# A hybrid pooling and linear-attention trunk: hand-ordered stages with barriers, against a list-scheduled rewrite with wider blocks and folded weights

## The chip, the cores and the metric

One Trainium2 chip, all 8 cores of it, one batch element on each core. The time is that of the slowest core, in device microseconds (us). A program on all cores has two states. In the slow one, the cores of a die show a lower granted TensorE clock and the run is longer: of the changed kernel's four runs one took 2278.8 us, with a mean clock of 0.92 to 0.94 on one die, against 2212.47 to 2216.9.

## The reference, cut to what matters

Four layers on 2048 tokens plus 16 meta tokens, width 1024, inner width 2048. Layers 0 and 2 are pooling mixers, layers 1 and 3 gated linear attention (GLA).

```python
def pool_mixer(h, w_in, w_grp, scale, w_out):
    u, z = split(h @ w_in)                                   # 2048 each
    t = trailing_mean(u, windows 2, 4, 8, 16 by group) - u   # linear in u, along the tokens
    y = einsum('blgc,gcd->blgd', t, w_grp)                   # 512 x 512 in each of 4 groups
    return (y * scale * silu(z)) @ w_out

def gla_mixer(h, w_in, w_gate2, b_gate, head_norm, w_out):   # 4 heads, chunk by chunk
    cum = cumsum(log_sigmoid(glr @ w_gate2 + b_gate) / 16)   # within a chunk
    qe, ke = q * exp(cum), k * exp(-cum)
    o = tril(qe @ ke.T) @ v + qe @ S
    S = exp(g_tot) * S + (k * exp(g_tot - cum)).T @ v
    return (rmsnorm_head(o) * head_norm * silu(z)) @ w_out

h = h + mixer(rmsnorm(h, norm), ...)                         # per layer; a last rmsnorm at the end
```

Two facts carry the change. The window mean runs along tokens and `w_grp` along channels, so `w_grp` may be applied before the window, that is, multiplied into `w_in` once. And the next layer's `rmsnorm` of a token tile needs only that tile's finished `h`.

## The kernel before

Every engine has its own instruction list. The order in each list is the order in which the program states its operations. A record of readers and writers of each buffer puts in the semaphore waits. Ahead of each layer stands a norm pass over all 17 token tiles, between barriers:

```python
def prepass(gvec_ap, gla):
    ...
    P.barrier()
    hnbs = [hnb, arena[:, 0:512].bitcast(BF16)]     # two buffers for the normalised tile, in turn
    ...
    for i in range(NT):
        pT = body(i)          # DVE: h * rstd * gain -> hnbs[i % 2]; PE: 8 transposes into bank i % 2
        if i + 2 < NT:
            stats(i + 2)      # ACT: square with sum, ln, exp
        evac(i, pT)           # ACT: PSUM -> hnT

def pool_layer(li, ui0):
    prepass(pool_norm[j:j + 1, :], False)
    ...
    P.barrier()
    def stageB(bi):           # the group matmul, 16 instructions per 256 tokens
        for oc in range(4):
            for fc in range(4):
                ins = e.matmul(py[:, oc, 0:n], lhsT=Wg[:, fc, ...], rhs=T[par][:, fc, 0:n], ...)
```

## Time and profile before

| | before |
|---|---|
| median of 3 runs | 2314.25 us (2313.78 to 2317.47) |
| TensorE busy, profiled run | 2144.0 us, 93% of 2317.0 |
| until the first projection | 89.6 us |
| three norm passes between layers | some 94 us |
| pool block, 256 tokens | 12.19 us |
| GLA, 128 tokens | 9.00 us |

The lines behind the table stand in the prediction. The columns are the engine and line that waited, what it waited for, then the total us, the number of times and the longest.

```profile
PE ps L377 <- DVE hnb L368: 86.4, 19, 18.5
PE ps L532 <- ACT arena L476: 15.2, 6, 2.8
```

The first line is the norm pass (line 377 is its transposes), 86.4 us in 19 waits, most of it at the start. Nothing else comes near. Within the layers TensorE hardly waits: the time is the work itself, and the way to a shorter time is less of it, and no passes in between.

### The profile page before, as it was taken

To read this page: it belongs to the slowest core of one execution; us is meant where nothing else is said; L and a number is where in the kernel's file an instruction comes from. 1 tells how busy PE (TensorE), PEld (TensorE's weight loads), DVE (VectorE), ACT (ScalarE), POOL (GpSimd) and SP (SyncE) were. 2 spreads that over 40 slices of the span, in tenths; PEclk is the share of its full clock that TensorE was granted. 3 is DMA by queue.
4 is the path that set the end of the run, shared out by engine and by line. 5 is a ranking of instruction groups with operands and counts; after the bars stand their busy time and mean duration, and the time that the engine had idled before them with its cause. 6 is when DMAs were issued, how large, how long until landed. Compare 5 with 4: busy or idle time off the path is not lost.

```text
span 2317.0 us, 60097 instructions; the slowest of 8 cores (2307.8 to 2317.0 us)
## 1 busy us (share of the span) xinstructions
PE 2144.0 (93%) x22136; PEld 1563.1 (67%) x22136; DVE 1420.2 (61%) x2844; ACT 1168.2 (50%) x2579; POOL 360.4 (16%) x254
## 2 busy tenths in 40 slices
PE   1599999997999999999979999999799999999997
PEld 1477767675776776766657777777567677677675
DVE  3354544455777776767773544444657777677787
ACT  3321111235766676667763111113557676676787
POOL 0012234560000000000001133456200000000000
PEclk9999999998999999999979999999899999999998
DMA  9303040404004004030030030313400210400011
GB/s 220 68 12 63 3 65 1 74 11 73 2 2 75 2 4 72 2 59 9 2 65 12 1 65 1 65 21 54 74 11 2 42 34 2 75 2 2 29 57 65
DMA packets 14801, 86.67 MB, mean 37 GB/s; under 512 B 2498, under 2 KB 2498, under 8 KB 6324
## 3 DMA queue, kind: packets, MB, share of 16 engines
q0 software_dynamic: 9664, 63.31, 16.8%
q1 hardware_dynamic: 4852, 19.51, 2.5%
q8 instruction: 184, 3.01, 0.5%
q14 instruction: 101, 0.83, 0.1%
HBM read 137.47 MB, written 8.39 MB: 63 GB/s over the span
## 4 chain that ended last, share of the span: by engine, by line
PE 85%; DVE 4%; ACT 4%; issue 4%; DMA 2%; another core or an unknown queue 1%; DVEq 0%; POOL 0%; ACTq 0%; SPq 0%; POOLq 0%
PE ps L467 20%; PE ps L713 10%; PE ps L555 10%; PE ps L728 10%; PE ps L846 9%; PE ps L742 9%; PE ps L532 6%; PE ps L806 2%; PE ps L787 2%; DMA W<-wpack 2%; PE ps L783 1%; PE ps L680 1%; PE ps L377 1%; PE ps L829 1%
## 5 line engine op out<-in xcount | busy, mean ns | idle before, releaser
L467 PE MATMUL ps<-hnT,W 128*128 128x256 bf16 (+1 forms) x4608 | 476.1, 263 | 11.8 <-DVE arena L537 9.0
L467 PEld LDWEIGHTS ps<-hnT,W 128*128 128x128 bf16 x4608 | 416.2, 98 | 77.2 <-issue 17.1
L484 POOL TENSOR_TENSOR arena<-arena 128x1048 f32<-128x1048 f32 (+9 forms) x180 | 323.2, 1796 | 610.9 <-ACT arena L478 552.3
L537 DVE SCALAR_TENSOR_TENSOR arena<-ps,pscale,arena 128x256 bf16<-128x256 f32 (+1 forms) x288 | 131.4, 456 | 407.6 <-PE ps L532 384.0
L478 ACT ACTIVATE arena<-ps 128x1024 f32<-128x1024 f32 (+1 forms) x72 | 67.4, 936 | 417.3 <-PE ps L467 417.2
L846 PE MATMUL ps<-W,arena 128*128 128x512 bf16 (+1 forms) x1088 | 263.1, 386 | 0.0
L713 PE MATMUL ps<-hnT,W 128*128 128x128 bf16 (+1 forms) x4352 | 260.6, 217 | 0.0
L728 PE MATMUL ps<-W,hnT 128*128 128x512 bf16 (+1 forms) x1088 | 260.5, 383 | 0.0
L742 PE MATMUL ps<-hnT,W 128*128 128x128 bf16 (+1 forms) x4352 | 256.9, 216 | 0.0
L555 PE MATMUL ps<-W,arena 128*128 128x512 bf16 (+1 forms) x1088 | 255.3, 389 | 0.0
L713 PEld LDWEIGHTS ps<-hnT,W 128*128 128x128 bf16 x4352 | 244.5, 99 | 0.2
L742 PEld LDWEIGHTS ps<-hnT,W 128*128 128x128 bf16 x4352 | 236.7, 97 | 0.5
L850 DVE SCALAR_TENSOR_TENSOR h<-ps,arena,h 128x512 f32<-128x512 f32 (+1 forms) x272 | 203.7, 749 | 33.9 <-PE ps L846 8.0
L731 ACT ACTIVATE arena<-ps 128x512 bf16<-128x512 f32 (+1 forms) x136 | 81.1, 597 | 282.1 <-PE ps L728 279.3
L796 DVE SCALAR_TENSOR_TENSOR arena<-ps,hnorm,arena 128x128 bf16<-128x128 f32 (+1 forms) x544 | 187.0, 344 | 58.9 <-DVE arena L796 1.6
L298 POOL DMA_DIRECT2D W<-wpack x64 | 34.3, 547 | 1025.0 <-PE ps L829 932.0
L728 PEld LDWEIGHTS ps<-W,hnT 128*128 128x128 bf16 (+1 forms) x1088 | 105.2, 98 | 130.6 <-issue 6.9
L559 DVE TENSOR_TENSOR h<-h,ps 128x512 f32<-128x512 f32 (+1 forms) x272 | 180.5, 683 | 16.6 <-PE ps L555 3.4
L555 PEld LDWEIGHTS ps<-W,arena 128*128 128x128 bf16 (+1 forms) x1088 | 107.4, 100 | 122.7 <-issue 17.5
L812 DVE SCALAR_TENSOR_TENSOR arena<-arena,ps 128x512 f32<-128x512 f32 x240 | 178.3, 743 | 12.9 <-DVE arena L812 0.5
L846 PEld LDWEIGHTS ps<-W,arena 128*128 128x128 bf16 (+1 forms) x1088 | 100.6, 98 | 101.6 <-issue 6.0
L532 PE MATMUL ps<-arena,W 128*128 128x256 bf16 (+1 forms) x1152 | 140.0, 277 | 23.1 <-ACT arena L476 15.2
(96 smaller groups left out, 2778.6 us busy)
## 6 DMA issues: line engine op xcount, KB each, us to landing
W<-wpack POOLq DMA_DIRECT2D x56, 1024.0 KB, 16.9
h<-x SPq DMA_DIRECT2D x8, 1024.0 KB, 33.4
out<-h SPq DMA_DIRECT2D x16, 512.0 KB, 2.6
W<-wpack POOLq DMA_DIRECT2D x8, 512.0 KB, 19.8
gbc<-pool_norm SPq DMA_DIRECT2D x2, 512.0 KB
gbc<-gla_norm SPq DMA_DIRECT2D x2, 512.0 KB
gbc<-final_norm SPq DMA_DIRECT2D x1, 512.0 KB
arena<-cst POOLq DMA_DIRECT2D x1, 128.0 KB, 6.5
```

The source lines that it names most:

```text
L467: ins = e.matmul(dst[:, fc, 0:n], lhsT=Wuz[:, kc, off + fc * 128:off + (fc + 1) * 128], rhs=hnT[:, kc, c0:c0 + n], start=(kc == 0), stop=( ...
L484: add = lambda dst, a, b: (lambda e: e.tensor_tensor(out=dst, in0=a, in1=b, op=ALU.add))
L532: ins = e.matmul(py[:, oc, 0:n], lhsT=Wg[:, fc, oc * 128:(oc + 1) * 128], rhs=T[par][:, fc, 0:n], start=(fc == 0), stop=(fc == 3))
L555: ins = e.matmul(po[0:nt, :], lhsT=Y[par][:, oc, cc:cc + nt], rhs=Wo[:, oc, half * 512:(half + 1) * 512], start=(oc == 0), stop=(oc == 3))
L559: P.op("dve", lambda e, half=half, nt=nt, ti=ti, po=po: e.tensor_tensor(out=h[0:nt, ti, half * 512:(half + 1) * 512], in0=h[0:nt, ti, half ...
L713: ins = e.matmul(pq[:, idx * 2 + dc, 0:n], lhsT=Wm[:, kc, dc * 128:(dc + 1) * 128], rhs=hnT[:, kc, c0:c0 + n], start=(kc == 0), stop=(kc = ...
L728: ins = e.matmul(pv[0:n, :], lhsT=hnT[:, kc, c0:c0 + n], rhs=Wv[:, kc, :], start=(kc == 0), stop=(kc == 7))
L742: ins = e.matmul(pz[:, ec, 0:n], lhsT=Wz[:, kc, ec * 128:(ec + 1) * 128], rhs=hnT[:, kc, c0:c0 + n], start=(kc == 0), stop=(kc == 7))
L796: P.op("dve", lambda e, ec=ec: e.scalar_tensor_tensor(out=yT[par][:, ec, 0:n], in0=po[:, ec, 0:n], scalar=hnorm[:, hd * 4 + ec:hd * 4 + ec ...
L812: P.op("dve", lambda e, dc=dc: e.scalar_tensor_tensor(out=S[:, dc, :], in0=S[:, dc, :], scalar=Eq[par][:, dc, n - 1:n], in1=pS[dc][:, :], ...
L846: ins = e.matmul(pout[0:n, :], lhsT=yT[par][:, ec, 0:n], rhs=Wo[:, ec, half * 512:(half + 1) * 512], start=(ec == 0), stop=(ec == 3))
L850: P.op("dve", lambda e, half=half, pout=pout: e.scalar_tensor_tensor(out=h[0:n, ti, half * 512:(half + 1) * 512], in0=pout[0:n, :], scalar ...
```

## The change

The intent is to drop work that TensorE needn't do and to let the norm of the next layer run inside the last group or head of this one. A rewrite; its core:

```diff
-    def barrier(self, engs=("pe", "act", "dve")):
+    def schedule(self):        # list scheduling of all operations with modelled durations
+        ...                    # an engine takes the ready operation that the program states first
-        P.op("pe", mmg, [bT[par], Wb[s][1]], PB(0, 1))           # group matmul per block
+    def fold(ui):              # w_in[:, group] @ w_grp, once for each group: 32 matmuls of 512
-        blocks = [(0, NMETA, [0])] + [(NMETA + NB * b, NB, ...)]  # meta, 8 x 256; GLA: 17 tiles
+BLOCKS = [([0, 1], 0, 144)] + [... 7 x 256 ...] + [([16], 1936, 128)]
-                        e.matmul(pcum[:, dc, 0:n], lhsT=lhi[...], rhs=tri[0:n, 0:n], ...)
+                    e.tensor_tensor_scan(out=Eq[...], data0=ones[...], data1=la[...], ...)  # DVE
-        S = exp(g) * S + kd.T @ v          # k scaled by exp(g_tot - cum)
+        S = el_prev * S + ke.T @ v         # k as it is; the decay goes into the copy that is read
+                    act([A["S"], b_el], [A["Sb"]], Sb[...], S[...], AF.Copy, scale=el[:, dc, k:k + 1])
-    hnbs = [hnb, arena[:, 0:512].bitcast(BF16)]
+    hnb = [sb("hnb0", [128, D], BF16)]      # one buffer, also where the square's output goes
-                  [(lambda q, k=k: q.dma_start(out=h[:, 1 + 2 * k:3 + 2 * k, :], ...   # x: 8 x 1 MB
+        dma("sp", "x%d" % i, h[:, i - 1, :], xv[:, i - 1, :], ...)                     # x: 16 x 512 KB
```

In the new GLA layer:

```python
def chunk(k_, k, t_, o, m):                          # one tile of 128 tokens in one head
    mm([b_ke, b_qe], [bank[4]], ...scores...)        # PSUM bank 4
    tr([b_ke, b_const], [bank[4]], ...k...)          # PSUM bank 4
    ...                                              # output: bank 5; state, projection: banks 6, 7
    if hd == 3:
        after_tile(li, t_)

def after_tile(li, t_):
    norm_tile(t_, 4)                                 # the next layer's norm: transposes in bank 4
```

## The prediction

> **What bounds the kernel now.** I read the page first: busy time by engine, the 40 slices, the chain that ended last. Then the trace: windows by stage, the matmul timeline for the cost of one instruction, the timeline of a norm pass for the cost of its hops.
>
> ```profile
> PE 2144.0 (93%) x22136; PEld 1563.1 (67%) x22136; DVE 1420.2 (61%) x2844; ACT 1168.2 (50%) x2579; POOL 360.4 (16%) x254
> PE   1599999997999999999979999999799999999997
> PE 85%; DVE 4%; ACT 4%; issue 4%; DMA 2%; another core or an unknown queue 1%; DVEq 0%; POOL 0%; ACTq 0%; SPq 0%; POOLq 0%
> ```
>
> TensorE is the bound: 85% of the chain is matmuls. The holes are the first slice and three dips between layers. The windows give their size (start, a pool group, norm pass, a GLA head, norm pass; columns: length, then busy time of PE, weight loads, DVE, ACT, POOL, granted clock, DMA share, GB/s):
>
> ```profile
> 0.00:89.60 89.60, 16.54 (x136) 12.70 (x137) 31.06 (x37) 34.15 (x71) 5.68 (x14) 1.00 0.83 186
> 307.70:417.00 109.30, 106.26 (x858) 79.55 (x857) 51.35 (x104) 18.25 (x27) 49.52 (x32) 0.95 0.22 35
> 529.50:562.00 32.50, 20.81 (x274) 16.24 (x273) 21.80 (x18) 23.31 (x45) 0.53 (x1) 0.88 0.50 92
> 870.00:1025.00 155.00, 154.17 (x1845) 109.55 (x1843) 110.31 (x237) 105.89 (x256) 2.11 (x4) 0.99 0.18 30
> 1191.00:1219.60 28.60, 16.56 (x138) 12.72 (x139) 22.39 (x18) 18.85 (x24) 0.53 (x1) 0.50 0.48 78
> ```
>
> 89.6 us pass before the first projection; a norm pass is 28 to 33 us of little matmul work, after which the clock is 0.50; inside the layers TensorE has no air. Its steady price, from the chain in order of time:
>
> ```profile
> 121.91 3.45 PE ps L555 x16
> 125.37 6.99 PE ps L467 x64
> 134.10 3.45 PE ps L555 x16
> ```
>
> L467 streams 256 columns: 6.99/64 = 109.2 ns each. L555 streams 512: 3.45/16 = 215.6. The block period is 134.10 - 121.91 = 12.19 us, of which 12.19 - 6.99 - 3.45 = 1.75 is the group matmul (16 x 109.2). With 128 columns, L713 x32 starts at 1174.99 and its successor at 1176.78: 55.9 ns. With 16 columns 29.7 (563.38 to 564.33, x32), with one 27.5. GLA's period is 9.00 us per 128 tokens (632.31 to 641.31).
>
> Counting the program and multiplying: 5256 x 109.2 + 11536 x 55.9 + 3520 x 215.6 + 1280 x 29.7 + 544 x 27.5 = 2031 us. The span is 2317, so 286 us are not matmul streaming: some 80 at the start, about 58 in three norm passes (94 us less some 36 of transposes and gate-input matmuls), the rest (near 148) group and head boundaries, half-clock stretches behind them, and the tail.
>
> **What the Trainium skill says.** "TensorE: Matmul & The Clock Gate", section "Wait — 56ns, not 53.3ns?": back-to-back spacing is N/2.4 ns + about 2.5 ns. The trace agrees: 109.2, 215.6, 55.9. Same page, "Part 1: The HAM clock gate": after an idle window of about 3.4 us the array runs at half clock until it has been busy for as long. The trace agrees: clock 0.50 at 1191 to 1219.6, and behind a 2.5 us gap at 190.37 sixteen matmuls of 256 columns took 3.57 us. The same section warns of a peak-current limiter at 13/16 of the clock once three cores of a die run dense matmuls. The trace shows it only in short bursts: 0.81 at 450 to 455 us on this core, none on die 0. "ScalarE: Activation LUTs", "What ACT_TABLE_LOAD costs": a per-partition pointer operand adds about 93 ns; L733's 398 ns at 128 columns against 365 for 256 columns without one (L682) fits.
>
> **The change, part by part.**
>
> Group matmul folded. It drops 1152 matmuls (1024 x 109.2 + 128 x 29.7 = 116 us) and adds 8 folds of 32 x 215.6 = 6.9 us, 55 us. Net -61.
>
> 256-token blocks. GLA's q, k, z go from 128 columns to 256: 8192 x 55.9 = 458 becomes 3584 x 109.2 + 512 x 62.5 (144 columns, an estimate by the formula) + 512 x 55.9 = 452: only -6. The pool layers' first and last block are 144 and 128 instead of 256: +5. The meta tile's own 16-column projections go (1024 x 29.7 = -30), and its output projection turns from 128 matmuls of 512 columns into 224 of 16: -21.
>
> Gates transposed with scan: the 512 + 32 cumulative-sum matmuls go (-30), ScalarE and VectorE take over. Gate input on wider blocks: a few us at most. The parts add up to -143 or so.
>
> All counted from the built program: 7392 of 256, 3648 of 512, 3616 of 128, 1056 of 144, 488 of 16, 512 of 1: 1890 us. Streaming falls by 140.
>
> Other engines, at the durations of before. ScalarE in GLA per 256 tokens: gate 0.91 + 0.63 + 1.26, v 1.19, z by exp-ln-exp 3.70, kd 0.73, square 1.16, the scaled state copy 4 x 0.72, head norm 0.89: 13.4 us. VectorE: q, k 1.39, z 4 x 0.484, mask 0.57, y 1.38, state 2.97, output 3.0, scan 4 x 0.34 (estimate): 12.6. TensorE: 64 x 109.2 + 36 x 215.6 + 32 x 55.9 + 2 x 109.2 + 8 x 27.5 = 17.0. So both lie beside it. In the fourth head each tile adds a norm: ScalarE +5.5 per block, 18.9 against TensorE's 17.9: there ScalarE binds by 1 us a block, some 8 us in one layer. Pool block: TensorE 12.19 - 1.75 = 10.44; ScalarE 5.6; VectorE 6.6; GpSimd with window 16 four adds of 2.03 plus a copy, 8.4, close but under.
>
> No barriers, norms in the stream: the three passes (58 us) and most boundaries go. Their transposes remain in the 1890.
>
> The start. This I expect NOT to improve. In the built order TensorE's first fold stands behind the transposes of all 16 tiles, and the changed kernel has one normalised-tile buffer, which is also the junk output of the square. So a tile's chain must close before the next begins. Its hops, here before the second pool layer:
>
> ```profile
> 1191.85 1.06 ACT L318 ACTIVATE hnT<-h 128x1024 bf16<-128x1024 f32 x1 [3.80 <-DVE h L850]
> 1193.09 0.29 ACT L342 ACTIVATE lnv<-ssb,epsc 16x1 f32<-16x1 f32 x1
> 1193.47 0.20 ACT L344 ACTIVATE rstd<-lnv 16x1 f32<-16x1 f32 x1
> 1193.85 1.27 DVE L368 SCALAR_TENSOR_TENSOR hnb<-h,rstd,gbc 16x1024 bf16<-16x1024 f32 x1 [2.09 <-ACT rstd L344]
> 1195.05 1.27 DVE L368 SCALAR_TENSOR_TENSOR arena<-h,rstd,gbc 128x1024 bf16<-128x1024 f32 x1
> 1196.46 1.01 PE L377 MATMUL ps<-ident,arena 128*128 128x128 bf16 x8 [0.84 <-DVE arena L368]
> 1197.56 1.02 ACT L386 ACTIVATE hnT<-ps 128x1024 bf16<-128x1024 bf16 x1 [1.57 <-PE ps L377]
> ```
>
> Square to ln 1.24, to exp 0.38, to the scaling 0.38, to the transposes 1.41, to the eviction 1.10, and 0.90 until ScalarE can start the next square (82.62 to 83.52): 5.4 us at half clock. Sixteen tiles take 87 us from the arrival of the first, about 12 us (a 1 MB chunk of x is used at 15.9 now; the first 0.5 MB should be 4 us earlier). So the first fold starts near 99 us, where projections started at 89.6. In between TensorE does only the transposes and one block's z, 9 us of its 1890.
>
> **Sum.** 99 for the start, 1881 of streaming, tail about 14 (now 10.9 us from the last output matmul at 2306.1 to the end, plus the wait before it), three layer changes at about 6 (the shared arena makes the gates wait for the last window), 8 for the fourth head, clock loss 12 (now 33 us at 0.81 cost 6), and 1 to 1.5% stalls (24) where the fixed order was laid out with other durations than the chip's. Total 99 + 1881 + 14 + 18 + 8 + 12 + 24 = 2056, say 2055.
>
> **The rivals.** One: the schedule does not hold; every late producer stalls an in-order TensorE by the same amount in every block. For it: out-projections share two PSUM banks (four before), GpSimd at 8.4 of 10.44. Against: ScalarE at 79%, VectorE at 74% in GLA leave room. With 5% stalls: about 2125. Two: the limiter. Dense matmul without pauses on eight cores could hold the 13/16 clock; over everything that would be 1881 x 0.23 = 430 us more, and the kernel slower. For it: the bursts in the pool layer. Against: 600 us of 99% busy GLA at 0.99, pool at full clock for most of its time. I take a fifth of the stream on one die as the bad case: 2140. Three: the start chain is hidden (data arrives late anyway, or warm transposes): x is there by about 62 us (estimate: 9.4 MB at the measured sharing), so it would end at 70: 2025.
>
> **Range and chances.** Good case 1990 (start 75, stalls under 1%), bad case 2125. For less than 2% gain all rivals must strike at once. Faster 0.97, same 0.02, slower 0.01.
>
> **What would show it.** First fold near 99 us with TensorE idle before; busy sums of the matmul lines near 1890 of streaming; no dips between layers in the slices; clock above 0.97; in a pool block a period of 10.44, in GLA 17.0. Wrong if the fold starts before 80 us, if blocks repeat a gap, or if the clock sits at 0.81.

## More of the kernel before

GLA works on one tile of 128 tokens at a time. It forms the cumulative sum of the gates by matmuls with a triangular matrix, and keeps each kind of product in a PSUM bank of its own for the whole head:

```python
patt = bank(4)[:, 0:128]                      # scores
pkdT = bank(2)[:, 0:128].bitcast(BF16)        # transposed k, shares with the v projection
po   = bank(5)...                             # output
pS   = [bank(6), bank(7)]                     # state update and output projection
```

## The result, and the profile after

| | before | after |
|---|---|---|
| median | 2314.36 us (4 runs) | 2215.44 us (4 runs, 2212.47 to 2278.8, one of them slow) |
| ratio of fast runs | | 0.9566, 95% interval 0.9551 to 0.9581 |
| TensorE's steady work starts (first projection before, first fold after) | 89.6 us | 118.5 us |
| TensorE busy, profiled run | 93% | 89% |

Ratios are the mean time of one kernel's fast runs over that of the other's fast runs of the same rounds, so they are not quite the ratio of the medians quoted. The kernel became faster, by 4.3%. The prediction was 2055 us with a range to 2125; it is 160 us too low. (One block's projection already runs at 84.33 us in the changed kernel, among the norms, as the prediction has it; the rest stands behind the fold.)

The page of the changed kernel: busy times, TensorE and its clock in 40 slices, the chain that ended last.

```profile
PE 1978.5 (89%) x16712; PEld 1406.1 (63%) x16712; DVE 1327.1 (60%) x2151; ACT 1365.1 (62%) x2903; POOL 428.5 (19%) x468
...
PE   0289999987999999996775999999989999999997
...
PEclk9899999999999999998876789999999999999998
...
PE 79%; DVE 6%; issue 5%; ACT 4%; POOL 3%; DMA 2%; SPq 0%; DVEq 0%; ACTq 0%; POOLq 0%
```

TensorE's busy time fell by 166 us (the matmul count promised some 140), yet it is busy for a smaller share. The slices, 55.4 us each, say where: the first two are nearly empty, and the nineteenth to twenty-second (997 to 1218 us), which were to be at 9, stand at 5 to 7 with a clock well under full. The chain has fewer matmuls and more of everything that feeds them. By windows (start, a stretch of GLA, the fourth head of the first GLA layer; columns as in the prediction):

```profile
0.00:118.50 118.50, 20.00 (x177) 16.48 (x178) 23.13 (x26) 44.04 (x88) 6.82 (x17) 0.88 0.59 132
560.00:720.00 160.00, 159.58 (x1419) 111.82 (x1418) 113.59 (x216) 111.06 (x249) 6.18 (x24) 1.00 0.16 28
1100.00:1200.00 100.00, 67.10 (x484) 44.10 (x484) 40.82 (x67) 46.34 (x100) 1.61 (x5) 0.72 0.09 17
```

The middle line is what was predicted for the whole stream: 159.58 of 160 us busy at full clock. The last is not: two thirds busy, clock 0.72, and ScalarE, which was to bind there, is busy for 46 of 100 us. What TensorE waited for is mostly one thing, at the start (some 82 us of it) and in the fourth head:

```profile
PE ps L409 <- DVE hnb L432: 136.6, 38, 9.7
```

Line 409 is the transposes of a normalised tile. The pool layer is as predicted. Two corresponding lines, one block apart:

```profile
159.58 5.40 PE L401 MATMUL ps<-hnT,W 128*128 128x256 bf16 x48
...
170.02 5.34 PE L401 MATMUL ps<-W 128*128 128x512 bf16 x24
```

170.02 - 159.58 is 10.44 us, the predicted period to the digit (only what follows is a fold here).

**The start.** TensorE's own lines, from the first x tile to the first fold:

```profile
26.98 1.01 PE L409 MATMUL ps<-ident,hnb 128*128 128x128 bf16 x8 [9.68 <-DVE hnb L432]
...
40.37 1.01 PE L409 MATMUL ps<-ident,hnb 128*128 128x128 bf16 x8 [7.00 <-DVE hnb L432]
...
62.00 1.01 PE L409 MATMUL ps<-ident,hnb 128*128 128x128 bf16 x8 [4.37 <-DVE hnb L432]
67.38 1.01 PE L409 MATMUL ps<-ident,hnb 128*128 128x128 bf16 x8 [4.37 <-DVE hnb L432]
...
118.46 8.68 PE L401 MATMUL ps<-W 128*128 128x512 bf16 x32
```

Look first at 62.00 and 67.38: 5.38 us from tile to tile with TensorE idle for 4.37, the chain of the single buffer as predicted (5.4). But the first tile comes at 26.98, not at about 12, and tiles 3 to 5 come 7.7 to 8.6 us apart (only one of them is shown): they wait for data. The first tile's square itself starts at 23.43, released by x's arrival. So the fold is at 118.46, not 99.

**The fourth head.** One tile's loop, from one norm's transposes to the next (all engines, time order; cut to the lines of the chain):

```profile
1020.20 1.01 PE L409 MATMUL ps<-ident,hnb 128*128 128x128 bf16 x8 [3.21 <-DVE hnb L432]
...
1021.31 1.02 ACT L426 ACTIVATE hnT<-ps 128x1024 bf16<-128x1024 bf16 x1 [2.94 <-PE ps L409]
...
1023.64 0.28 PE L401 MATMUL ps<-qe,ke 128*128 128x128 bf16 x2
...
1030.02 1.61 DVE L432 SCALAR_TENSOR_TENSOR h<-ps,rs,h 128x512 f32<-128x512 f32 x2 [2.18 <-ACT rs L426]
1031.72 1.06 ACT L426 ACTIVATE hnb<-h 128x1024 bf16<-128x1024 f32 x1 [1.80 <-DVE h L432]
...
1032.96 0.29 ACT L426 ACTIVATE rstd<-ssb,epsc 128x1 f32<-128x1 f32 x1
1033.35 0.20 ACT L426 ACTIVATE rstd<-rstd 128x1 f32<-128x1 f32 x1
1033.65 1.29 DVE L432 SCALAR_TENSOR_TENSOR hnb<-h,rstd,gbc 128x1024 bf16<-128x1024 f32 x1 [2.03 <-ACT rstd L426]
...
1035.09 1.01 PE L409 MATMUL ps<-ident,hnb 128*128 128x128 bf16 x8 [4.57 <-DVE hnb L432]
1036.19 1.02 ACT L426 ACTIVATE hnT<-ps 128x1024 bf16<-128x1024 bf16 x1 [2.64 <-PE ps L409]
...
1037.36 0.37 PE L401 MATMUL ps<-qe,ke 128*128 128x128 bf16 x2 [1.26 <-ACT hnT L426]
```

The reader follows the releasers. The normalised tile is transposed at 1020.20 and evicted at 1021.31; then come this tile's scores at 1023.64, its output and projection, `h` at 1030.02, the square (1031.72), two small activations, the scaling (1033.65), the transposes (1035.09), the eviction (1036.19), and only then the next scores, at 1037.36, which waited for `ACT hnT`: the eviction of the *previous* tile's norm. Scores have no business with that; what they share is PSUM bank 4. So the program states a ring for each tile: scores, output, projection, `h`, norm, transposes, eviction, next scores, all behind one another. Two tiles, one block of 256, take 1054.19 - 1020.20 = 34.0 us instead of 17 to 19. List scheduling can't help: it reorders only what the buffers leave free.

**The clock.** While the ring runs, TensorE's idle time costs clock too: over the whole execution the clock records of the eight cores add up to 120 to 157 us at 0.50, in e1 below, where the ring is open, to 46 to 79. Besides, four cores show a clock of 0.81 from the last part of that head on. Core 7, then core 3, in the same 20 us:

```profile
1240.00:1260.00 20.00, 20.00 (x128) 13.75 (x127) 11.25 (x14) 9.64 (x17) 4.01 (x4) 0.81 0.00 1
```

```profile
1240.00:1260.00 20.00, 20.00 (x154) 14.86 (x153) 12.44 (x16) 10.46 (x19) 4.03 (x4) 1.00 0.00 1
```

Both are full; core 7 runs at 0.81. The clock records of this execution add up to 114 to 128 us at 0.81 on cores 0, 1, 6 and 7 and none on the other four. The four end at 2210.9 to 2214.9 us, the other four at 2195.1 to 2200.7: some 14 us (2213.1 and 2198.6 on average), which may be read as its price (an estimate from the two means).

### The profile page after: what moved, and what is told of

It reads as the page before. It is cut to its first block, busy times and chain, and to the rows that moved or that the text cites. A ratio compares the mean times of both kernels' runs of the same rounds, so it can differ in the third digit from the quotient of the medians.

```text
span 2214.9 us, 46775 instructions; the slowest of 8 cores (2195.1 to 2214.9 us)
## 1 busy us (share of the span) xinstructions
PE 1978.5 (89%) x16712; PEld 1406.1 (63%) x16712; DVE 1327.1 (60%) x2151; ACT 1365.1 (62%) x2903; POOL 428.5 (19%) x468
## 4 chain that ended last, share of the span: by engine, by line
PE 79%; DVE 6%; issue 5%; ACT 4%; POOL 3%; DMA 2%; SPq 0%; DVEq 0%; ACTq 0%; POOLq 0%
PE ps L401 77%; DVE hnb L432 2%; DMA h<-x 2%; PE ps L409 2%; POOL SB L437 2%; ACT hnb L426 1%; DVE h L432 1%; POOL SA L437 1%; DVE Y L437 1%; ACT gs L426 1%; ACT rstd L426 1%; ACT hnT L426 1%; DVE S L432 0%; DVE SB L432 0%; DVE sz L432 0%
## 5 line engine op out<-in xcount | busy, mean ns | idle before, releaser
L401 PE MATMUL ps<-hnT,W 128*128 128x256 bf16 (+1 forms) x9216 | 988.0, 265 | 12.9 <-ACT vb L426 5.9
L401 PE MATMUL ps<-W,Y 128*128 128x512 bf16 x1024 | 249.8, 386 | 15.8 <-DVE Y L437 9.3
L401 PE MATMUL ps<-W,hnT 128*128 128x512 bf16 x1088 | 261.6, 385 | 0.6 <-DVE sz L432 0.6
L437 DVE TENSOR_TENSOR h<-h,ps 128x512 f32<-128x512 f32 x256 | 175.0, 684 | 129.7 <-PE ps L401 127.6
L401 PE MATMUL ps<-W,yT 128*128 128x512 bf16 x1024 | 250.0, 387 | 0.3 <-DVE S L432 0.3
L432 DVE SCALAR_TENSOR_TENSOR h<-ps,rs,h 128x512 f32<-128x512 f32 x256 | 191.0, 746 | 98.5 <-ACT rs L426 56.8
L426 ACT ACTIVATE Sb<-S,el 128x512 bf16<-128x512 f32 x256 | 183.3, 716 | 47.0 <-DVE S L432 29.9
L432 DVE SCALAR_TENSOR_TENSOR S<-S,el,ps 128x512 f32<-128x512 f32 x240 | 176.9, 737 | 58.7 <-PE ps L401 57.4
L426 ACT ACTIVATE sg<-sg 128x512 f32<-128x512 f32 (+2 forms) x288 | 167.9, 585 | 23.8 <-ACT sg L426 0.8
L426 ACT ACTIVATE gs<-gs 128x512 f32<-128x512 f32 (+2 forms) x288 | 166.6, 579 | 7.4
```

Of the source, the lines that this page charges most:

```text
L401: ins = e.matmul(o_, lhsT=l_, rhs=r_, start=st, stop=sp_)
L426: P.op("act", lambda e: e.activation(out=out_, in_=in_, func=func, scale=scale, **kw), reads, writes, dur, 130.0)
L432: P.op("dve", lambda e: e.scalar_tensor_tensor(out=out_, in0=a, scalar=s, in1=b, op0=op0, op1=op1), reads, writes, dve_dur(free_n(out_)) + ...
L437: P.op(eng, lambda e: e.tensor_tensor(out=out_, in0=a, in1=b, op=op), reads, writes, dve_dur(n) if eng == "dve" else n * 1.7 + 100.0, 100.0)
```

## The experiments

Theory A: the fourth head is bound by the ring through bank 4. Theory B, its rival: ScalarE is short of time in the fourth head (the prediction's own reason), so another bank buys little. Theory C: the start is bound by the single normalised buffer and by x's arrival. Theory D, for the whole: the fixed order itself doesn't fit the chip's durations, and stalls everywhere. Runs were sent in three batches; before had medians of 2312.14 us in the first (e1 to e4) and 2319.05 us in the other two. The changed kernel was not run again. Gains are given against its median, and they agree with the ratios to before: for e1, (0.9566 - 0.9125) x 2312 = 102 us, where the medians say 104.

### e1: the norm's transposes in another bank

```diff
 def after_tile(li, t_):
+    nb_ = 4 if li % 2 == 0 else 3          # GLA: bank 3, which only the gates use
-    norm_tile(t_, 4)
+    norm_tile(t_, nb_)                     # the meta tile's norm likewise
```

> Changed kernel, but the norm of the next layer inside a GLA layer transposes into PSUM bank 3 (the gates' bank) instead of bank 4 (the scores' and kd transposes' bank). Theory A, the shared bank 4 makes a loop tile by tile (scores of the next tile wait for the eviction of this tile's norm): the fourth head of the first GLA layer falls from 34.3 us a block to about 19 to 20, some 120 us in all, total near 2095. Rival B, the chain through the one normalised-tile buffer is the limit: block stays above 30, total above 2185. Rival C, ScalarE is the bound there: block stays, total within 1% of 2215. The start stays at 118.

Measured: 2111.48 us (2108.24 to 2112.17 fast, one slow run of 2167.7), ratio 0.9125 [0.9109, 0.9141]. That is 104 us less than the changed kernel. One block of after (34 us), then three blocks of e1 in the fourth head:

```profile
1020.20:1054.19 33.99, 22.26 (x146) 13.86 (x147) 14.54 (x25) 16.93 (x35) 0.37 (x2) 0.80 0.00 1
```

```profile
1001.57:1060.27 58.70, 53.24 (x426) 34.51 (x431) 42.66 (x71) 48.43 (x104) 2.48 (x8) 1.00 0.10 17
```

58.70 us for three blocks is 19.6 each. Each needs 16.1 us of ScalarE (48.43/3) and 17.7 of TensorE (53.24/3). The work per block is that of after (16.93 of ScalarE), in little more than half the time. In after the 16 tiles' transposes span 986.74 to 1233.64 us, in e1 979.33 to 1135.75 (32.9 and 20.9 us a block over the whole head): 91 us of the 104 are in this head. The rest has the size of what the 0.81 clock took in after (14 us): e1's profiled run shows no 0.81 on any core, and against the four cores of after that show none either (2198.6 us on average) e1's eight (2104.4) gain 94. A holds, B falls. So does the rival in the expectation that the single normalised buffer sets this block: e1 keeps that buffer.

### e10: half the dose

Only every second tile leaves bank 4, so that a ring is opened once in two tiles.

```diff
+    nb_ = 4 if li % 2 == 0 or t_ % 2 == 0 else 3
```

> Changed kernel with bank 3 only for odd tiles in GLA layers, bank 4 for even ones: half the dose. If each pass through bank 4 costs its own wait: a block of the fourth head between 25 and 28 us, total 2155 to 2175 (half of the 104 us that bank 3 brought). If one pass a block is enough to hold the loop: total above 2190. If the odd tiles alone made the loop: near 2111.

Measured: 2157.03 us (2156.28 to 2159.15), 0.9311 [0.9294, 0.9328], as expected. Two blocks:

```profile
997.56:1051.58 54.02, 42.42 (x316) 29.12 (x317) 29.10 (x49) 34.46 (x70) 0.74 (x4) 0.85 0.00 1
```

The block took 27.0 us (transposes at 997.56, 1024.53, 1051.58), midway between 34.0 and 19.6. The gain is 58 us of e1's 104. This is the check that it is the shared bank, dose by dose, and not a lucky order.

### e2: a second buffer for the normalised tile

In the pool layers' arena 2 KB per partition are free, so norms made there (the start, and the last group) take two buffers in turn.

```diff
+                 ("hn2", 2048, BF16, [128, 1024])]
+    def nbuf(i):
+        return (T["hn2"], A["hn2"]) if in_pool[0] and i % 2 == 1 else (hnb[0], b_hnb[0])
```

> Changed kernel with a second normalised-tile buffer for the norms made in pool layers and at the start (none in GLA). Theory A, the 5.38 us chain on one buffer sets the start: tiles then follow at 2.5 to 3 us or as x arrives, the first fold falls from 118 to about 75 to 85 (x and the weights have then landed), total near 2175 to 2185, fourth head of the first GLA layer unchanged at 34 us a block. Rival, the loads set the start: fold stays above 110 and total at 2215.

Measured: 2161.04 us (2159.92 to 2161.09 fast, one slow run of 2286.02), 0.9342 [0.9322, 0.9362]: 54 us less, more than expected, though the fold came later than the 75 to 85 us expected. The start, where the tiles stood 5.38 us apart:

```profile
59.30 1.01 PE L410 MATMUL ps<-ident,hnb 128*128 128x128 bf16 x8 [1.81 <-DVE hnb L433]
62.03 1.01 PE L410 MATMUL ps<-ident,hn 128*128 128x128 bf16 x8 [1.73 <-DVE hn L433]
65.02 1.01 PE L410 MATMUL ps<-ident,hnb 128*128 128x128 bf16 x8 [1.98 <-DVE hnb L433]
```

They are now about 3 us apart, from the time when the data is there, and the first fold is at 92.87 instead of 118.46: 26 us. By the first norm in the fourth head the lead is 35 us (951.39 against 986.74): another 9 to 10 lie where the pool layer's last group makes the next layer's norms. The remaining 19 come later, and the traces tell two parts of it apart. Until the meta tile's norm in the second pool layer the lead grows from 35 to 50 us (1482.07 against 1532.42); in that stretch lies after's 0.81 clock, of which this profiled run shows none on any core. Only some 5 come after it, with the second pass of norms. So some 40 of the 54 us belong to the buffer: against the four cores of after without 0.81 (2198.6 us) e2's eight (2156.4) gain 42. The fourth head is as slow as before.

### e3: both

> Both edits. If the two losses are separate they add: about 2215 - 120 - 38 = 2057, range 2040 to 2075. If the bank loop was only half of the fourth head's loss: above 2090.

Edit: e1 and e2 together. Measured: 2081.07 us median; the fast runs are 2066.12, 2066.62 and 2095.53 (in the last, two cores are 30 us longer at a lower clock; a fourth run was slow), hence a wide interval, 0.8977 [0.8901, 0.9052]. The expectation was 2057 from gains of 120 and 38; the gains measured, 104 and 54, give the same sum by chance. Two runs came within 10 us of it, the median misses the range. The two gains add up in these two runs, as those of separate faults would.

### e4: the same operations in the program's order

```diff
-        while left: ...           # list scheduling
+        for o in ops:
+            order[o.eng].append(o)
```

> Changed kernel with each engine's instructions in the order in which the program states them, no list scheduling. If the order is what hides the chains: every pool block then waits for its own window chain (10.4 us of matmuls plus 8 to 12), every GLA tile for its own scores, state and norm (8.5 plus about 8), total 3000 to 4200 us, slower than the kernel before. If the dependencies alone already let it overlap: within 10% of 2215.

Measured, one look: 4473.65 us (4347.51 to 4521.61), all three runs in the slow state. What TensorE waited for, the first and a later line of the list:

```profile
PE ps L355 <- DVE Y L391: 630.3, 72, 13.1
PE ps L363 <- DVE am L391: 450.7, 124, 6.5
```

Each block waits for its own window and its own masked scores, since the program states a block from top to bottom. The size must not be read from the slow cores; but cores 0 and 1 of the profiled run, which show no 0.81, end at 4245.0 and 4242.1 us. So the order of the list is worth about a factor of two, more than was expected. Theory D falls as the main cause: inside the layers the order leaves TensorE 159.58 of 160 us busy. At the layer changes small waits remain (below).

### e6: x in pieces of 1 MB

Two changes were mixed in the start: the buffer, and the size of x's transfers. This undoes the second alone in the changed kernel.

```diff
-    for i in range(1, NT):
-        dma("sp", "x%d" % i, h[:, i - 1, :], xv[:, i - 1, :], [], [hb[i]], 524288)
+    for k in range(8):
+        dma("sp", "x%d" % k, h[:, 2 * k:2 * k + 2, :], xv[:, 2 * k:2 * k + 2, :], ..., 1048576)
```

> Changed kernel with x in eight transfers of two tiles (rows of 8 KB) as before the change, instead of sixteen of one tile (rows of 4 KB). Theory: x shares the DMA engines with the weight queue in pieces, so halved rows halved its share; first transposes fall from 27.0 to about 16 to 19 us, then the 5.38 us chain binds at once, first fold at 105 to 110 instead of 118.5, total 2203 to 2209. Rival, the row length doesn't matter: first transposes at 27, total 2215.

Measured: 2203.54 us (2202.05 to 2205.21), 0.9511 [0.9493, 0.953]: 12 us less. The second and third tile:

```profile
33.75 1.01 PE L409 MATMUL ps<-ident,hnb 128*128 128x128 bf16 x8 [4.37 <-DVE hnb L432]
39.13 1.01 PE L409 MATMUL ps<-ident,hnb 128*128 128x128 bf16 x8 [4.37 <-DVE hnb L432]
```

The gaps of 8 us are gone; from the first tile on it is the bare chain of 5.38, and the fold is at 109.96. The total and the fold came as expected; the first tile did not (28.37, expected at 16 to 19). The Trainium skill, "DMA: Bandwidth & Descriptors", section "Queues, rings and completion order", says that each DMA engine takes turns between the queues that have work, packet by packet. The trace agrees. The two queues from 15 to 50 us, in the changed kernel, then here (the software queue carries the weights, the hardware queue x; packets, MB, the time that they took):

```profile
q0 software_dynamic: 675, 4.42, 74.6%
q1 hardware_dynamic: 674, 2.49, 26.9%
```

```profile
q0 software_dynamic: 590, 3.76, 64.3%
q1 hardware_dynamic: 589, 4.25, 37.1%
```

Each queue gets as many packets through as the other, and x's are rows of 4 KB in the first case and of 8 KB in the second. The edit also halves the number of transfers, so SyncE is done issuing them at 9 us instead of 54; that this matters too was not tested.

### e5 and e9: the start, with the loads in the order of need

e5 is e3 with x's first tiles and the first group's weights ahead of the rest, and the second group's load stated behind the first fold. (In the changed kernel the fold shares a buffer record with that later load, and so waits for it.)

```diff
-    DMA_NS_PER_BYTE = 1.0 / 200.0
+    DMA_NS_PER_BYTE = 1.0 / 330.0
+    load_x(1, 4, [])
     load_unit(0)
-    load_unit(1)
+    load_x(4, NT, [Wb[1][2]])
     ...
                     fold(0)
+                    gate1[0] = [hb[10]]     # the second group's weights wait for x tile 10
+                    load_unit(1)
```

> Both edits of before (bank 3, second buffer) plus loads in the order of need: three tiles of x with the first unit's weights, the other x tiles after the weights that the fold reads, the second unit's weights after tile 10 of x, and its load stated after the first fold, so that the fold no longer waits for it through the shared buffer name; the scheduler's transfer rate is set to 330 bytes per ns. Theory: the first fold falls from 93 to about 30 us and norms hide under matmuls; total 2066 - 60, between 1990 and 2020. Rival, x or its norms then starve the first blocks: the first unit shows gaps before its transposes and the total stays above 2040.

Measured: 2056.25 us (2053.88 to 2059.76), 0.8874 [0.8858, 0.8891]: a miss by 36 us. The fold came at 43.96 us, later than the 30 expected but 49 earlier than in e3, but the end of that layer only 15 us earlier (its last group's meta norm is at 378.76 us, in e3 at 393.84). In the first group the norms were now made just in time: the projections of a block waited 1.3 to 1.8 us for them. So part of the waiting moved from the first fold into the blocks behind it.

e9 states each norm two blocks ahead of its use, takes x in pieces of 1 MB, and starts the second group's load after all of x.

```diff
-                    norm_block(0, bi, 4 + bi % 2)
+                    for b2 in ... range(bi + 2, bi + 3):
+                        norm_block(0, b2, 4 + b2 % 2)
```

> The kernel with loads in order of need, with the norms of the first layer stated two blocks ahead of their use, x in 1 MB pieces, the second unit's weights after all of x. Theory: the 15 us instead of 49 that the early fold brought were lost to norms stated just in time (gaps of about 3 us a block in the first unit); with the norms ahead the first unit keeps near 10.4 plus 1 us a block, total 2015 to 2040. Rival, data arrives too late for it: gaps before the transposes remain, total 2050 or above.

Measured: 2030.65 us (fast runs 2026.64 to 2032.13, one slow of 2292.18), 0.8760 [0.8746, 0.8774]. As expected, and the fastest of all. The last wait before the first fold, the fold, and what follows it:

```profile
36.57 0.61 PE L410 MATMUL ps<-ident,hnb 128*128 128x128 bf16 x8 [0.59 <-DVE hnb L433]
37.01 7.07 PE L402 MATMUL ps<-W 128*128 128x512 bf16 x32
44.11 7.56 PE L402 MATMUL ps<-hnT,W 128*128 128x256 bf16 x80
```

TensorE is continuously busy from 37 us on; in the 140 us from 60 to 200 it is idle for 0.16 us. Which of e9's three edits brought how much of the 26 us over e5 was not separated.

### e7 and e8: the group matmul back

Both are e1 with the fold undone: one group matmul of 16 instructions per block, as before. In e7 its results rotate through the same four projection banks.

```diff
+                    for k in range(2):
+                        b = proj_bank()                       # e8: b = (3, 5)[k], and proj_bank has 3
+                        mm([A[Tn], Wb[s][3]], [bank[b]], ...group matmul...)
-                    fold(0)
```

> Bank 3 kernel (2111) with the fold undone: group matmul after the window as in the kernel before, scale on its eviction, u weights loaded as they are. Streaming +116 - 55 = +61 us: a pool block takes 12.2 us instead of 10.44. But no fold stands before the first block any more, so projections should start near 30 us beside the norms instead of at 118 and some 80 us come back at the start: total near 2090 (2065 to 2115). Rival, the start is bound by data or norms and not by the place of the fold: total near 2172.

Measured: fast runs of 2449.33 and 2450.99 us (the median of all four, 2504.5, mixes them with two slow ones), 1.0573 [1.0548, 1.0598], slower than before. A bad miss. TensorE's largest wait that e1 doesn't have, and two neighbouring lines of a block:

```profile
PE ps L402 <- DVE T L433: 119.5, 55, 5.6
```

```profile
221.25 3.66 PE L402 MATMUL ps<-hnT,W 128*128 128x256 bf16 x32
227.37 1.91 PE L402 MATMUL ps<-T,W 128*128 128x256 bf16 x16 [2.46 <-DVE T L433]
```

The group matmul (`T,W`) waits 2.46 us for the window's result. The next block's projections could be done in that time, but in the rotation their bank comes behind the group result's bank. It is theory A's fault again, made by my own edit: a shared bank turns the statement order into a ring. e8 gives the group matmul banks 3 and 5 for itself, which tests that.

> The fold undone again on the bank 3 kernel, but with banks 3 and 5 for the group matmul and a rotation of three banks for z and u, so that the next block's u no longer stands behind this block's group result in one rotation. Theory, the 2504 us of the first unfolded kernel came from that rotation (matmuls waited 119.5 us for the window's result, 55 times): a block falls to about 12.2 us, waits for the window's result under 30 us, total 2100 to 2150 (2111 + 61 - about 46 at the start, where work now runs beside the norms). Rival, the window chain itself makes an unfolded block long in this schedule: blocks of 14 us and more, total above 2250.

Measured: 2154.74 us (2150.23 to 2155.68), 0.9300 [0.9283, 0.9316], some 295 us less than e7's fast runs and a few us above what was expected. The wait for the window's result is nearly gone:

```profile
PE ps L402 <- DVE T L433: 5.5, 6, 2.4
```

Four blocks take 48.9 us (group matmuls at 337.95 and 386.87), 12.2 each as expected; in e7 two take 35.8 (357.15 to 392.96). So the assignment of the banks was the cause in e7. Against e1 the fold is worth 43 us where the prediction's sum says 61 (in that comparison the start and the number of projection banks differ too: without a fold to wait for, e8's first window projection is at 93.73 us, e1's behind the fold at about 127).

## Why the prediction was right and wrong, step by step

**Right.** The streaming: a pool block has the predicted 10.44 us, and in GLA from 560 to 960 us TensorE is busy for 398.7 of 400 us at clock 1.00. The start's mechanism: "a tile's chain must close before the next begins", 5.4 us, measured 5.38; and the start did not improve. The direction, and the absence of norm passes after the pool layers' last group as such (the pass of 32 us at half-empty TensorE no longer stands by itself in the trace).

**Wrong, and by far the largest: the term "8 for the fourth head".** The step reads: "there ScalarE binds by 1 us a block, some 8 us in one layer". It compared sums of busy time, engine by engine, and took the largest as the period. The period was that of a ring through all engines, 34.0 us a block, while ScalarE was busy for half of it. The ring is there because the norm's transposes and the scores share PSUM bank 4. e1 opens it with one added and two changed lines and gains 104 us; e10 opens half and gains 58. Even ScalarE's sum was too high: 16 to 17 us, not 18.9. That the block took 19.6 us once the ring was open is near the predicted 18.9 by luck: neither ScalarE nor TensorE (17.7) fills it. The prediction did this very sum of a ring's hops at the start, for the buffer of the normalised tile, and did not do it for the bank in the fourth head. The Trainium skill, "Perfetto Trace Analysis", "Matmuls", says that independent matmul groups should rotate through different PSUM banks so that the eviction of one overlaps the next group. The trace agrees, and adds a price for not doing it: 34.0 us against 19.6.

**Wrong in size: "99 for the start".** The chain was right, its beginning was not. "The first 0.5 MB should be 4 us earlier" took half the bytes for half the time; its square started at 23.43 us, not at 12, which is 11 us of the 20. Some 8 more are the waits of tiles 3 to 5 for data. The term measured 118.5. e6 takes away the second part (fold 8.5 us earlier, 12 us in the total), which was the transfer's size; it does not touch the first (square at 24.82), and what made the first tile late was not isolated.

**The clock term, 12 us,** was about right in size by luck and happened otherwise: 14 us or so, on four cores, from the end of the idle fourth head on. Why there and why on those cores is open. The mean clock, expected above 0.97, was 0.955 to 0.973. **The layer changes, 18 us,** were too low by some 20: TensorE is idle for 22 us between 400 and 560 (the first change) and for 14 between 1600 and 1760 (the third), in many waits of 1 to 3 us for window results, normalised tiles and their evictions, where 6 each were put down. Head, start and layer changes together (91 + 20 + 20) leave some 30 us of the 160 that no run assigns. About half may be in the head still: e1's 20.9 us a block against 18.9 make 16 us over eight blocks (an estimate).

**The rivals.** None of the three was what happened. The first ("every late producer stalls an in-order TensorE by the same amount in every block") has the right form, a repeated gap, but looked for it in the output projection's banks and at 5% everywhere; it was in one head, with twice the period of 17.0 us. Two small faults, removed, bring two of three fast runs to 2066 us, 11 above the prediction. That doesn't confirm its terms one by one: in that run the fold is at 93.44 us, not 99, and no core shows 0.81.

**Three readings in the prediction** are looser than it says, without weight in the sum. The clock of 0.50 is that of the third norm pass itself; in the first it is 0.88. The gap at 190.37 us (2.47 us) is shorter than the idle window of 3.4 us that it is said to agree with. And L733 and L682 differ in their columns and in what they read too, so they don't isolate what the pointer operand costs.

## What to carry to other kernels

When operations of two stages come to share a PSUM bank or a buffer, write down the ring of who must finish before whom and add up its hops; compare that with the engines' sums, and take the larger. A scheduler reorders only what the buffers leave free, so after such a rewrite look first for slices with a low TensorE share and ask what the waiting instruction shares with the one that released it. And when a start is shortened, look at what must then keep up: a fold 49 us earlier was 15 us at the end of the layer. With the norms made ahead, x in larger pieces and the second load later (e9), the end of the layer came another 30 us earlier.

## What the Trainium skill lacked or had wrong

- "TensorE: Matmul & The Clock Gate", "Part 1: The HAM clock gate": it describes the 13/16 limiter as taking a whole die once three of its cores run dense matmuls, and holding while the load lasts. Here it came in pieces and on some cores: 114 to 128 us on cores 0, 1, 6 and 7 and none on 2 to 5 in the changed kernel's profiled run; 85 us on cores 4 and 5, 55 on 6 and 7 and none on die 0 in e9. From 560 to 720 us all eight cores of the changed kernel ran dense GLA, busy for 158.1 to 159.6 of the 160 us, at 1.00.
- "Perfetto Trace Analysis", "Matmuls": it names rotation through banks for independent groups, not that a rotation in statement order can close a ring itself. e7, with four rotating banks, took 2450 us in its fast runs; e8, with the group matmul's two banks set apart from a rotation of three, 2154.74.
- "DMA: Bandwidth & Descriptors", "Queues, rings and completion order": it states the turns between queues, but not what they cost a queue with smaller rows. With as many packets from each queue (674 and 675), rows of 4 KB moved 2.49 MB in 35 us, beside 4.42 MB of weights in rows of up to 8 KB; rows of 8 KB moved 4.25. Transfers of half the size cost 12 us of 2215 here.
